# A down projection of a decoder block in Strassen's form, two feature tiles at a time

## The chip, the cores and the metric

The kernel runs on one core of one Trainium2 chip. The time is device microseconds of one launch; three runs of the kernel before give a median of 775.1 us (775.02 to 776.29). The profile is one more execution, which took 774.55 us.

## The reference, cut to what matters

One decoder block on 512 tokens of width 1024, all in float32: norm, two attention mixers side by side, gates, an output projection, then the dense feed-forward part, and a last norm. The change lies in the last product of the feed-forward part, `@ w_down`.

```python
h = rmsnorm(x, norm_ffn[layer])
x = x + (jax.nn.silu(h @ w_gate[layer]) * (h @ w_up[layer])) @ w_down[layer]
return rmsnorm(x, norm_final)
```

`h` is 512 x 1024, `w_gate` and `w_up` are 1024 x 2816, and `w_down` is 2816 x 1024. So the last product has 512 rows (tokens), 1024 columns and a sum over 2816 features.

## The kernel before, in words

**Three matmuls for a float32 product.** TensorE is fed the type fp32r. A float32 operand m is split in two: hi is a copy of m by ScalarE in that type, and lo = m - hi is a subtraction. A product is then hi·hi + lo·hi + hi·lo, three matmuls into one PSUM bank (`mm3`, L200 to L203; L201, L202 and L203 are the three).

**How weights come in.** A `Chunk` (L132 to L178) takes a weight tile of 128x512 float32 (256 KB) by a DMA on SyncE's queue into one of RAW=5 buffers (L153); ScalarE writes `whi` (L172), and VectorE and GpSimd take turns at `wlo` (L164, `PLO` at L108). There are WB=8 buffers each of whi and wlo, so that no split is made until TensorE has read the tile that lay in its buffer.

**Stages.** Up to about 405 us the projections, the two attentions and the output projection; from there the gate and up products (L1007 to L1034, to 645 us); the down projection (L1038 to L1055, 645 to 765 us); and the end of the last norm. The span is 772.8 us.

**Gate and up.** The loop takes feature tiles of 128 features in pairs. For each pair and each of the two weights, TensorE does 2 x 8 `mm3`; the result is features x tokens, a tile of 128x512. VectorE scales g and u (L1016, L1025), ScalarE applies Silu (L1017), VectorE multiplies u by g (L1026), and the result is split in ah (ScalarE, L1032) and al (VectorE, L1033). These 22 pairs of tiles stay in SBUF as the stationary operands of what follows.

**Down.** Eight PSUM banks, `po[b, h]`, hold the output: four blocks b of 128 tokens, two halves h of 512 columns. For each of the first 18 features f, two weight tiles come (h = 0, 1), and TensorE does `mm3` for all b and h, 24 matmuls; the last `LAST = 4` features are done block by block, so that the norm of a block can begin while the next is computed. Then `x1[b][h]`, the residual, is added (L1057), squared and summed (ScalarE, L1060), scaled, and stored.

Engines run their own instructions in the order in which the scheduler of the framework has put them, and wait for one another through semaphores. That order is fixed when the kernel is built; it follows the order of the code and a priority of each instruction, and what the framework's own estimates hold to be ready. Buffers come from pools: `kp` has K2=39 slots of 128x512 under the tag `k2`, in which the operands h2 of gate and up (16 slots), the residual x1 (8) and some of the ah and al lie.

Of the kernel before, what the change touches and what calls it, by code (L numbers as in the profile page):

```python
# [38 lines left out]
def hybrid_block(ctx: ExitStack, tc: tile.TileContext, x, norm_mix, w_in, w_up_a, w_up_b, w_out,  # L39
# [968 lines left out]
    for f in range(0, NF, 2):
        G = []
        W = chunk(wg, [(f * P, 256)])  # L1010
        for j in range(2):
# [7 lines left out]
        W = chunk(wu, [(f * P, 256)])  # L1019
        for j in range(2):  # L1020
# [6 lines left out]
            if f < NFP:  # L1027
                hi, lo = fp.tile([P, 512], F32R, name=f"ah{f + j}"), fp.tile([P, 512], F32R, name=f"al{f + j}")
            else:
                tag = "y" if f + j >= NF - 2 else "rp" if f + j == NF - 3 else "k2"  # L1030
                hi, lo = [kp.tile([P, 512], F32R, tag=tag, bufs={"y": YB, "rp": 2, "k2": K2}[tag], name=f"a{n}{f + j}") for n in "hl"]
            nc.scalar.activation(hi, u, AF.Copy)  # L1032
            nc.vector.tensor_tensor(lo, u, hi.bitcast(F32), op=ALU.subtract)  # L1033
            actT.append((hi, lo))  # L1034
# [5 lines left out]
    LAST = 4  # L1040
    W = {}
    for f in range(NF):
        for h in range(2):
            W[f, h] = chunk(wd[f * P:(f + 1) * P], [(512 * h, 512)], kts=1, per=1)[0]
        if f < NF - LAST:
            for b in range(NB):
                for h in range(2):
                    mm3(po[b, h], (actT[f][0][:, b * P:(b + 1) * P], actT[f][1][:, b * P:(b + 1) * P]), W[f, h], f == 0, False)
    for i in range(2):
        nc.gpsimd.tensor_scalar(gF[:, i * 512:(i + 1) * 512], gF[:, i * 512:(i + 1) * 512], 0.0625, 1.0, op0=ALU.mult, op1=ALU.mult)  # L1050
    for b in range(NB):
        v = None
        for h in range(2):
            for f in range(NF - LAST, NF):
                mm3(po[b, h], (actT[f][0][:, b * P:(b + 1) * P], actT[f][1][:, b * P:(b + 1) * P]), W[f, h], False, f == NF - 1)  # L1055
# [3 lines left out]
            jk = fp.tile([P, 512], F32, tag="g", bufs=3, name="jk")  # L1059
# [50 lines left out]
```

## Time and profile before

| | before |
|---|---|
| median of 3 runs | 775.1 us (775.02 to 776.29) |
| profiled execution | 774.55 us |
| its span (first to last instruction) | 772.8 us |
| mean granted TensorE clock | 0.993 of full speed |
| TensorE busy | 744.1 us, 96% |
| VectorE / ScalarE / GpSimd busy | 435.6 / 352.6 / 281.4 us |
| HBM read / written | 68.46 MB / 2.10 MB |

Busy time of TensorE is the time in which at least one matmul is between its start and its modelled end; matmuls overlap, so that one lasts 0.39 us while the next starts after 0.227. Where the table of stretches has a granted clock of 1.00, TensorE ran at its upper level (2.4 GHz); 0.50 is the lower level (1.2 GHz).

### The profile page before, as it was taken

The page shows a single profiled execution, that of the slowest core. Times are in us where ns is not written, and L with a number is a line of the kernel's source. Part 1 is how long each engine was busy: PE and PEld are TensorE (multiplying, and loading weights), DVE is VectorE, ACT ScalarE, POOL GpSimd, SP SyncE. Part 2 cuts the span into 40 slices and gives each one's busy share as a digit, 9 for nine tenths or more (in the row PEclk, how much of TensorE's full clock was granted, in tenths as well). Part 3 has the DMA queues.
Part 4 walks back from the last instruction along what each step waited for, and adds up shares of the span by engine and source line. Part 5 has one row for each costly group of instructions (what it writes and reads, how often), then busy time and mean ns, then how long its engine had stood idle before and what let it go on. Part 6 is the DMA issues. An engine that isn't in the chain of part 4 may idle for free.

```text
span 772.8 us, 10634 instructions
## 1 busy us (share of the span) xinstructions
PE 744.1 (96%) x3621; PEld 625.2 (81%) x3621; DVE 435.6 (56%) x910; ACT 352.6 (46%) x722; POOL 281.4 (36%) x263
## 2 busy tenths in 40 slices
PE   8988998988999999999999999999999999999995
PEld 7977887886888888888887888888888888888884
DVE  5789989997766557765334344344433343222235
ACT  7366566655666667533425333333333333121233
POOL 2653656645545455422121222222222222222223
PEclk9999999999999999999999999999999999999999
DMA  8352433322432221533232332233223333323202
GB/s 278 80 137 54 102 91 88 89 76 69 117 88 70 73 66 55 176 112 107 82 106 59 109 103 88 83 109 109 84 85 105 109 101 90 105 86 109 83 14 109
DMA packets 68502, 74.53 MB, mean 96 GB/s; under 512 B 5392, under 2 KB 55584, under 8 KB 68448
## 3 DMA queue, kind: packets, MB, share of 16 engines
q1 hardware_dynamic: 68448, 73.86, 32.7%
q8 instruction: 28, 0.46, 0.2%
q14 instruction: 26, 0.21, 0.1%
HBM read 68.46 MB, written 2.10 MB: 91 GB/s over the span
## 4 chain that ended last, share of the span: by engine, by line
PE 82%; DVE 10%; ACT 3%; issue 2%; DMA 1%; SPq 0%; POOL 0%; ACTq 0%; DVEq 0%; POOLq 0%
PE o L202 5%; PE u L203 5%; PE o L203 5%; PE u L202 5%; PE u L201 5%; PE o L201 5%; PE g L203 5%; PE g L202 5%; PE g L201 5%; PE gate L201 3%; PE gate L202 3%; PE gate L203 3%; PE x L203 2%; PE x L201 2%; PE x L202 2%
## 5 line engine op out<-in xcount | busy, mean ns | idle before, releaser
L164 POOL TENSOR_TENSOR wlo<-raw,whi 128x512 fp32r<-128x512 f32 (+1 forms) x156 | 206.1, 1331 | 386.6 <-ACT whi L172 376.4
L172 ACT ACTIVATE whi<-raw 128x512 fp32r<-128x512 f32 (+1 forms) x242 | 149.6, 625 | 240.1 <-PE u L203 70.9
L164 DVE TENSOR_TENSOR wlo<-raw,whi 128x512 fp32r<-128x512 f32 x86 | 71.9, 836 | 128.3 <-ACT whi L172 127.8
L201 PE MATMUL g<-h2h,whi 128*128 128x512 f32 x176 | 68.7, 390 | 0.0
L203 PE MATMUL g<-h2l,whi 128*128 128x512 f32 x176 | 68.7, 390 | 0.0
L202 PE MATMUL g<-h2h,wlo 128*128 128x512 f32 x176 | 68.6, 390 | 0.0
L201 PE MATMUL u<-h2h,whi 128*128 128x512 f32 x176 | 68.5, 389 | 0.0
L202 PE MATMUL u<-h2h,wlo 128*128 128x512 f32 x176 | 68.5, 389 | 0.0
L203 PE MATMUL u<-h2l,whi 128*128 128x512 f32 x176 | 68.5, 389 | 0.0
L201 PE MATMUL o<-whi,ah 128*128 128x512 f32 x176 | 68.5, 389 | 0.0
L202 PE MATMUL o<-whi,al 128*128 128x512 f32 x176 | 68.5, 389 | 0.0
L203 PE MATMUL o<-wlo,ah 128*128 128x512 f32 x176 | 68.5, 389 | 0.0
L684 POOL TENSOR_SCALAR sm<-sm,st 128x256 f32<-128x256 f32 (+3 forms) x64 | 40.0, 632 | 62.4 <-DVE st L683 52.1
L201 PE MATMUL gate<-hTh,whi 128*128 128x512 f32 x128 | 51.6, 403 | 0.0
L203 PE MATMUL gate<-hTl,whi 128*128 128x512 f32 x128 | 50.2, 392 | 0.0
L202 PE MATMUL gate<-hTh,wlo 128*128 128x512 f32 x128 | 50.1, 391 | 0.0
L679 ACT ACTIVATE sm<-sm,st 128x256 f32<-128x256 f32 (+3 forms) x64 | 35.6, 557 | 23.3 <-DVE st L678 23.1
L1025 DVE TENSOR_TENSOR u<-u,rb 128x512 f32<-128x512 f32 x22 | 15.2, 692 | 52.4 <-PE u L203 52.4
L201 PE MATMUL slot<-hTh,whi 128*128 128x512 f32 x104 | 41.7, 401 | 1.8 <-DVE va L563 1.1
L201 PE MATMUL proj<-whi,hTh 128*128 128x256 f32 (+1 forms) x128 | 38.4, 301 | 2.8 <-DVE va L563 1.2
L202 PE MATMUL slot<-hTh,wlo 128*128 128x512 f32 x104 | 40.8, 392 | 0.0
L203 PE MATMUL slot<-hTl,whi 128*128 128x512 f32 x104 | 40.7, 391 | 0.0
(268 smaller groups left out, 1627.0 us busy)
## 6 DMA issues: line engine op xcount, KB each, us to landing
raw<-in_w_in SPq DMA_DIRECT2D x54, 256.0 KB, 3.0
raw<-in_w_gate SPq DMA_DIRECT2D x44, 256.0 KB, 2.9
raw<-in_w_up SPq DMA_DIRECT2D x44, 256.0 KB, 2.9
raw<-in_w_down SPq DMA_DIRECT2D x44, 256.0 KB, 2.8
x<-in_x SPq DMA_DIRECT2D x16, 256.0 KB, 4.0
raw<-in_w_in SPq DMA_DIRECT2D x32, 128.0 KB, 2.5
raw<-in_w_out SPq DMA_DIRECT2D x16, 256.0 KB, 2.6
sw<-raw SPq DMA_DIRECT2D x50, 64.0 KB, 2.0
```

What stands on the lines that cost most here:

```text
L164: eng.tensor_tensor(lo, raw, hi.bitcast(F32), op=ALU.subtract)
L172: nc.scalar.activation(hi, raw, AF.Copy)
L201: nc.tensor.matmul(o, l[0], r[0], start=start, stop=False)
L202: nc.tensor.matmul(o, l[1], r[0], start=False, stop=False)
L203: nc.tensor.matmul(o, l[0], r[1], start=False, stop=stop)
L679: nc.scalar.activation(sm, sm, AF.Exp, bias=st[:, 0:1], scale=-1.0, accum_out=st[:, 1:2])
L684: nc.gpsimd.tensor_scalar(sm, sm, st[:, 2:3], 1.0, op0=ALU.mult, op1=ALU.mult)
L1025: nc.vector.tensor_tensor(u, p_, rb2, op=ALU.mult)
```

## The change

Nine of the eleven pairs of feature tiles of the down projection (the first 18 features) are computed in Strassen's form (Winograd's variant). For a pair, the activations are seen as a 2x2 matrix of blocks: two halves of the tokens (256 each) by two feature tiles; the weights as a 2x2 matrix: two feature tiles by two column halves. Seven block products take the place of eight; each block product is two token blocks of `mm3`, six matmuls.

What stands for the operands:

- In the gate and up loop, the products u·g of a pair go to one tile `ops` of eight parts of 256 tokens (L1042 in the changed file), and four VectorE subtractions or additions of 128x256 make S1, S2, S3 and S5. (A11, A22) and (S1, S2) are split in hi and lo and stay in SBUF, as before (three pairs in the pool `k2`, the others in `fp`); A12, S3 and S5 (128x768 float32, 384 KB) are written to DRAM, unsplit. The tag `g` has 2 buffers in place of 3.
- **Phase 1** does four of the seven products of all nine pairs, into eight banks. Its weights are r11 and three sums, each made by one VectorE addition from the one before (L1101, L1103, L1105), and split.
- **Between the phases** four banks are copied to SBUF (c1, c5) and two more are added to (V), and the four copied are started anew.
- **Phase 2** does the other three products. For each pair it reads `ra` (128x512) and `rb` (128x256) back from DRAM, splits them, takes three weight tiles from DRAM once more and makes one sum.
- Then the parts are added to the residual `x1`, and the last four features are done as before.

The lines of the diff that matter here:

```diff
-            nc.vector.tensor_tensor(u, u, G[j], op=ALU.mult)
+            if ops is not None:
+                to = ops[:, 0:5:4, :] if j else ops[:, 3:8:4, :]
+                nc.vector.tensor_tensor(to, halves(u), halves(G[j]), op=ALU.mult)
+                continue
...
+        A12, S3, S5, A11, A22, S1, S2, A21 = [ops[:, i] for i in range(8)]
+        nc.vector.tensor_tensor(S1, A21, A22, op=ALU.subtract)
+        nc.vector.tensor_tensor(S2, S1, A11, op=ALU.subtract)
+        nc.vector.tensor_tensor(S3, A11, A21, op=ALU.subtract)
+        nc.vector.tensor_tensor(S5, A12, S2, op=ALU.add)
+        spill = dram.tile([P, 768], F32, name=f"spill{pair}")
+        nc.sync.dma_start(spill, ops[:, 0:3].rearrange("p i c -> p (i c)"))
...
+    def wd_split(raw):
+        hi = wp.tile([P, WMAX], F32R, tag="whi", bufs=WB, name="whi")
+        lo = wp.tile([P, WMAX], F32R, tag="wlo", bufs=WB, name="wlo")
+        nc.scalar.activation(hi, raw, AF.Copy)
+        nc.vector.tensor_tensor(lo, raw, hi.bitcast(F32), op=ALU.subtract)
+        return hi, lo
+    def product(b0, h, a, o, w, start, stop):
+        for i in range(2):
+            c = slice(o + i * P, o + (i + 1) * P)
+            mm3(po[b0 + i, h], (a[0][:, c], a[1][:, c]), w, start, stop)
+    for pair in range(NS):
+        fl = (pair == 0, pair == NS - 1)
+        r11, r12, r22, r21 = wd_blocks(pair, ((0, 0), (0, 1), (1, 1), (1, 0)), pair == 0)
+        w11 = wd_split(r11)
+        nc.vector.tensor_tensor(r12, r11, r12, op=ALU.add)
+        u1 = wd_split(r12)
+        nc.vector.tensor_tensor(r22, r12, r22, op=ALU.add)
+        u2 = wd_split(r22)
+        nc.vector.tensor_tensor(r21, r22, r21, op=ALU.add)
+        u4 = wd_split(r21)
+        straight, sums = opA[pair]
+        product(0, 0, straight, 0, w11, *fl)
+        product(0, 1, sums, 0, u1, *fl)
+        product(2, 0, sums, 256, u2, *fl)
+        product(2, 1, straight, 256, u4, *fl)
+    c1, c5, V = [[k2(name=f"{n}_{i}") for i in range(2)] for n in ("c1", "c5", "V")]
+    for i in range(2):
+        nc.scalar.activation(c1[i], po[i, 0], AF.Copy)
...
+        nc.vector.tensor_tensor(V[i], po[2 + i, 0], c1[i], op=ALU.add)
+    for pair in range(NS):
+        ra, rb = k2(name="ra"), k2(name="rb")[:, :256]
+        nc.sync.dma_start(ra, opB[pair][:, 0:512])
+        nc.sync.dma_start(rb, opB[pair][:, 512:768])
+        a = store_pair(ra, "a", lambda n: k2(F32R, n))
+        s5 = store_pair(rb, "s5", lambda n: k2(F32R, n)[:, :256])
+        r21, r22, r12 = wd_blocks(pair, ((1, 0), (1, 1), (0, 1)), False)
+        w21 = wd_split(r21)
+        w22 = wd_split(r22)
+        nc.vector.tensor_tensor(r12, r12, r22, op=ALU.add)
+        u3 = wd_split(r12)
+        product(0, 0, a, 0, w21, pair == 0, False)
+        product(0, 1, s5, 0, w22, pair == 0, False)
+        product(2, 0, a, 256, u3, pair == 0, pair == NS - 1)
...
+    for i in range(2):
+        for o, y in ((x1[i][0], c1[i]), (x1[i][1], c5[i])):
+            if y is c5[i]:
+                nc.vector.tensor_tensor(y, y, V[i], op=ALU.subtract)
+            nc.vector.tensor_tensor(o, o, y, op=ALU.add)
...
-    for f in range(NF):
+    for f in range(NF - LAST, NF):
```

TensorE, the first rows of the down projection. Before, the tiles o_6468, o_6469, o_6470 and so on are the banks `po[0,0]`, `po[0,1]`, `po[1,0]` ..., and the stationary operands are ah and al of feature 0:

```order
L203 MATMUL u<-h2l_4583,whi 128x512
L201 MATMUL o_6468<-whi,ah_4751 128x512
L202 MATMUL o_6468<-whi,al_4752 128x512
L203 MATMUL o_6468<-wlo,ah_4751 128x512
L201 MATMUL o_6469<-whi,ah_4751 128x512
L202 MATMUL o_6469<-whi,al_4752 128x512
```

After, at the same place, o_6533 and o_6535 are `po[0,0]` and `po[1,0]`, o_6534 and o_6536 are `po[0,1]` and `po[1,1]`; a_3h, a_3l are hi and lo of (A11, A22), and a_5h, a_5l those of (S1, S2):

```order
L203 MATMUL u<-h2l_4583,whi 128x512
L201 MATMUL o_6533<-whi,a_3h 128x512
L202 MATMUL o_6533<-whi,a_3l 128x512
L203 MATMUL o_6533<-wlo,a_3h 128x512
L201 MATMUL o_6535<-whi,a_3h 128x512
L202 MATMUL o_6535<-whi,a_3l 128x512
L203 MATMUL o_6535<-wlo,a_3h 128x512
L201 MATMUL o_6534<-whi,a_5h 128x512
```

All rows of TensorE ahead of these are the same in both; a weight tile is now used by two banks in succession, where it was used by four. In the whole program TensorE has 54 rows fewer (3459 and 3405).

TensorE, from phase 1 to phase 2 (only in the changed kernel). o_6537 to o_6540 are the banks `po[2,0]`, `po[2,1]`, `po[3,0]`, `po[3,1]`; ah, al belong to `ra`, s5h, s5l to `rb`:

```order
L203 MATMUL o_6539<-wlo,a_5h 128x512
L201 MATMUL o_6538<-whi,a_3h 128x512
L202 MATMUL o_6538<-whi,a_3l 128x512
L203 MATMUL o_6538<-wlo,a_3h 128x512
L201 MATMUL o_6540<-whi,a_3h 128x512
L202 MATMUL o_6540<-whi,a_3l 128x512
L203 MATMUL o_6540<-wlo,a_3h 128x512
L201 MATMUL o_6533<-whi,ah 128x512
L202 MATMUL o_6533<-whi,al 128x512
L203 MATMUL o_6533<-wlo,ah 128x512
```

Between the last matmul of phase 1 and the first three of phase 2 stands nothing; the second reads al and the third reads wlo.

VectorE, in the down projection before: its subtractions for wlo (those that GpSimd does not do) stand alone until the first block of tokens is done.

```order
L1026 TENSOR_TENSOR u<-u,g 128x512
L1033 TENSOR_TENSOR al_6464<-u,ah_6463 128x512
L164 TENSOR_TENSOR wlo<-raw,whi 128x512 x18
L1057 TENSOR_TENSOR x_0_3977<-o_6468,x_0_3977 128x512
```

VectorE after, from the end of phase 1 on. c_0_7000 and c_1_7001 are c1, c_0_7002 and c_1_7003 are c5, the tiles x_ are parts of the residual:

```order
L1088 TENSOR_TENSOR wlo<-wraw,whi 128x512 x10
L1143 TENSOR_TENSOR x_0_3977<-x_0_3977,c_0_7000 128x512
L1143 TENSOR_TENSOR x_0_3981<-x_0_3981,c_1_7001 128x512
L1119 TENSOR_TENSOR V_7004<-o_6537,c_0_7000 128x512
L1119 TENSOR_TENSOR V_7005<-o_6539,c_1_7001 128x512
L1142 TENSOR_TENSOR c_0_7002<-c_0_7002,V_7004 128x512
L1142 TENSOR_TENSOR c_1_7003<-c_1_7003,V_7005 128x512
L1143 TENSOR_TENSOR x_1_3979<-x_1_3979,c_0_7002 128x512
L1143 TENSOR_TENSOR x_1_3983<-x_1_3983,c_1_7003 128x512
L1025 TENSOR_TENSOR al<-ra,ah 128x512
L1025 TENSOR_TENSOR s5l<-rb,s5h 128x256
L1088 TENSOR_TENSOR wlo<-wraw,whi 128x512 x2
```

Two V and six additions to c5 and x1 stand ahead of the first al and the first wlo of phase 2. GpSimd has no subtraction in either phase until the weights of the last four features.

## Rows read from the trace of the kernel before

**Rows 1.** From the page: busy time of each engine with its share of the span, and the chain of work that ended last, by engine.

```profile
PE 744.1 (96%) x3621; PEld 625.2 (81%) x3621; DVE 435.6 (56%) x910; ACT 352.6 (46%) x722; POOL 281.4 (36%) x263
...
PE 82%; DVE 10%; ACT 3%; issue 2%; DMA 1%; SPq 0%; POOL 0%; ACTq 0%; DVEq 0%; POOLq 0%
```

**Rows 2.** Busy time by stretch: gate and up, down projection, end. After the stretch and its length: busy us (and instructions) of PE, PEld, DVE, ACT, POOL, then the granted clock, the DMA share and GB/s.

```profile
416.20:645.00 228.80, 228.80 (x1011) 189.47 (x1010) 92.74 (x126) 80.09 (x128) 54.76 (x43) 1.00 0.33 96
645.00:765.00 120.00, 119.91 (x530) 98.95 (x528) 36.78 (x55) 32.82 (x59) 32.61 (x26) 1.00 0.26 85
765.00:772.80 7.80, 0.00 (x0) 0.00 (x0) 2.68 (x8) 1.65 (x4) 2.08 (x2) 0.77 0.33 122
```

**Rows 3.** The tile o (the eight banks of the down projection): its matmuls by line, with their count, duration in ns, and first and last start.

```profile
L201 PE MATMUL o<-whi,ah x176: 389/389/389, 645.1 to 764.1; 128*128 128x512 f32 x176
...
L202 PE MATMUL o<-whi,al x176: 389/389/389, 645.3 to 764.3; 128*128 128x512 f32 x176
...
L203 PE MATMUL o<-wlo,ah x176: 388/389/389, 645.5 to 764.5; 128*128 128x512 f32 x176
```

**Rows 4.** Timeline of TensorE as the down projection begins (start, duration).

```profile
644.62 0.39 PE L202 MATMUL u<-h2h,wlo 128*128 128x512 f32 x1
644.85 0.39 PE L203 MATMUL u<-h2l,whi 128*128 128x512 f32 x1
645.07 0.39 PE L201 MATMUL o<-whi,ah 128*128 128x512 f32 x1
645.30 0.39 PE L202 MATMUL o<-whi,al 128*128 128x512 f32 x1
```

**Rows 5.** The waits of the down projection: who waited for whom, us in total, times, longest.

```profile
DVE wlo L164 <- ACT whi L172: 73.6, 18, 4.3
ACT whi L172 <- PE o L202: 64.4, 16, 4.2
```

**Rows 6.** Groups by line and form: VectorE's subtraction of the weights in gate and up (first row), in the down projection (second) and in the whole kernel (third), busy us and mean ns of one; its smaller form of 256 columns elsewhere (fourth); ScalarE's split of weights from 412 us on (fifth); GpSimd's subtraction from 412 us on (sixth).

```profile
L164 DVE TENSOR_TENSOR wlo<-raw,whi 128x512 fp32r<-128x512 f32 x43 | 29.6, 689 | 29.6 <-ACT whi L172 29.1
...
L164 DVE TENSOR_TENSOR wlo<-raw,whi 128x512 fp32r<-128x512 f32 x19 | 23.3, 1228 | 73.6 <-ACT whi L172 73.6
...
L164 DVE TENSOR_TENSOR wlo<-raw,whi 128x512 fp32r<-128x512 f32 x86 | 71.9, 836 | 128.3 <-ACT whi L172 127.8
...
L698 DVE TENSOR_TENSOR ptl<-pT,pth 128x256 fp32r<-128x256 f32 x16 | 6.7, 418 | 2.6 <-ACT pth L697 2.4
...
L172 ACT ACTIVATE whi<-raw 128x512 fp32r<-128x512 f32 x123 | 77.7, 632 | 176.1 <-PE u L203 70.9 <-PE o L202 64.4 <-PE g L203 24.8
...
L164 POOL TENSOR_TENSOR wlo<-raw,whi 128x512 fp32r<-128x512 f32 x62 | 80.5, 1298 | 262.3 <-ACT whi L172 262.3
```

**Rows 7.** Timeline of VectorE: operations of 128x512 in succession, in gate and up.

```profile
624.23 0.69 DVE L164 TENSOR_TENSOR wlo<-raw,whi 128x512 fp32r<-128x512 f32 x1
624.84 0.68 DVE L1026 TENSOR_TENSOR u<-u,g 128x512 f32<-128x512 f32 x1
...
639.83 0.69 DVE L1025 TENSOR_TENSOR u<-u,rb 128x512 f32<-128x512 f32 x1 [4.03 <-PE u L203]
640.56 0.69 DVE L1026 TENSOR_TENSOR u<-u,g 128x512 f32<-128x512 f32 x1
```

**Rows 8.** One subtraction on GpSimd (first row) and one on VectorE (second) that overlap, in the down projection.

```profile
650.56 1.30 POOL L164 TENSOR_TENSOR wlo<-raw,whi 128x512 fp32r<-128x512 f32 x1 [4.59 <-ACT whi L172]
...
651.20 1.21 DVE L164 TENSOR_TENSOR wlo<-raw,whi 128x512 fp32r<-128x512 f32 x1 [2.53 <-ACT whi L172]
```

**Rows 9.** The last matmul of the down projection and the VectorE operation that reads its bank.

```profile
764.52 0.39 PE L203 MATMUL o<-wlo,ah 128*128 128x512 f32 x1
...
764.95 0.69 DVE L1057 TENSOR_TENSOR x<-o,x 128x512 f32<-128x512 f32 x1 [0.29 <-PE o L203]
```

**Rows 10.** The DMA engines as the kernel begins, in two stretches (the columns are those of rows 2), and the issues of the weights of the down projection: KB each and median us to landing.

```profile
0.00:20.00 20.00, 16.60 (x119) 15.30 (x120) 12.24 (x34) 14.70 (x41) 4.67 (x12) 1.00 0.79 272
8.00:16.00 8.00, 7.64 (x63) 7.23 (x63) 7.26 (x22) 7.00 (x23) 0.32 (x1) 1.00 1.01 378
...
raw<-in_w_down SPq DMA_DIRECT2D x44, 256.0 KB, 2.8
```

**Rows 11.** Timeline of TensorE at two places where it waits twice within a few us (in brackets the wait and what ended it), and after each of them the stretch that follows, in the columns of rows 2.

```profile
60.69 0.45 PE L613 MATMUL dots<-idx0h,idx 128*128 128x384 f32 x1 [1.81 <-ACT relu L861]
62.83 0.69 PE L613 MATMUL dots<-idx0h,idx 128*128 128x384 f32 x1 [1.17 <-ACT relu L861]
...
62.90:66.00 3.10, 3.10 (x13) 3.10 (x14) 3.07 (x5) 1.76 (x4) 2.01 (x2) 0.50 0.31 68
...
186.34 0.44 PE L613 MATMUL sc<-qk1A21h,qk0A 128*128 128x384 f32 x1 [1.40 <-DVE st L678]
188.22 0.50 PE L708 MATMUL y<-pth,va 128*128 128x512 f32 x1 [1.15 <-DVE st L683]
...
189.00:192.20 3.20, 3.20 (x15) 3.01 (x13) 1.54 (x7) 3.07 (x9) 2.94 (x3) 0.50 0.29 65
```

More of the change, by code (lines that the diff above doesn't have):

```diff
@@ L1004, in hybrid_block, with halves, store_pair @@
     gF = fp.tile([P, D], F32, name="gF")
-    actT = []
+    LAST = 4
+    NS = (NF - LAST) // 2
+    dram = ctx.enter_context(tc.tile_pool(name="dram", bufs=1, space=bass.MemoryType.DRAM))
+    opA, opB, act = [], [], {}
+    def halves(t):
+        return t.rearrange("p (i c) -> p i c", i=2)
+    def store_pair(m, name, alloc):
+        hi, lo = alloc(name + "h"), alloc(name + "l")
+        nc.scalar.activation(hi, m, AF.Copy)
+        nc.vector.tensor_tensor(lo, m, hi.bitcast(F32), op=ALU.subtract)
+        return hi, lo
     for f in range(0, NF, 2):
         G = []
+        pair = f // 2
         W = chunk(wg, [(f * P, 256)])
@@ L1019, in hybrid_block @@
         W = chunk(wu, [(f * P, 256)])
+        ops = fp.tile([P, 8, 256], F32, tag="ops", bufs=1, name="ops") if pair < NS else None
         for j in range(2):
@@ L1025, in hybrid_block @@
             nc.vector.tensor_tensor(u, p_, rb2, op=ALU.mult)
+            if ops is not None:
+                to = ops[:, 0:5:4, :] if j else ops[:, 3:8:4, :]
+                nc.vector.tensor_tensor(to, halves(u), halves(G[j]), op=ALU.mult)
+                continue
             nc.vector.tensor_tensor(u, u, G[j], op=ALU.mult)
[L1027 to L1034, printed above, removed]
+            i = f + j - (NF - LAST)
+            tag, bufs = (("y", YB) if i >= 2 else ("rp", 2) if i == 1 else ("k2", K2))
+            act[f + j] = store_pair(u, f"a{f + j}", lambda n: kp.tile([P, 512], F32R, tag=tag, bufs=bufs, name=n))
+        if ops is None:
+            continue
+        A12, S3, S5, A11, A22, S1, S2, A21 = [ops[:, i] for i in range(8)]
[5 more added lines that the diff above has]
+        nc.sync.dma_start(spill, ops[:, 0:3].rearrange("p i c -> p (i c)"))
+        opB.append(spill)
+        alloc = (lambda n: k2(F32R, n)) if pair < NSK else (lambda n: fp.tile([P, 512], F32R, name=n))
+        opA.append([store_pair(ops[:, i:i + 2].rearrange("p i c -> p (i c)"), f"a{pair}_{i}", alloc) for i in (3, 5)])
     nc.sync.dma_start(gF, bass.AP(tensor=norm_final.tensor, offset=norm_final.offset, ap=[[0, P], [1, D]]))
@@ L1039, in hybrid_block, with wd_blocks @@
     po = {(b, h): banks[2 * b + h](f"o{b}{h}") for b in range(NB) for h in range(2)}
-    LAST = 4
+    def wd_blocks(pair, which, from_wp):
+        res = []
+        for r, c in which:
+            t = wp.tile([P, WMAX], F32, tag="raw", bufs=RAW, name="raw") if from_wp else k2(name="wraw")
+            nc.sync.dma_start(t, wd[(2 * pair + r) * P:(2 * pair + r + 1) * P, 512 * c:512 * (c + 1)])
+            res.append(t)
+        return res
+    def wd_split(raw):
[3 more added lines that the diff above has]
+        nc.vector.tensor_tensor(lo, raw, hi.bitcast(F32), op=ALU.subtract)
+        return hi, lo
@@ new lines, in hybrid_block @@
+    c1, c5, V = [[k2(name=f"{n}_{i}") for i in range(2)] for n in ("c1", "c5", "V")]
+    for i in range(2):
+        nc.scalar.activation(c1[i], po[i, 0], AF.Copy)
+    for i in range(2):
+        nc.scalar.activation(c5[i], po[i, 1], AF.Copy)
+    for i in range(2):
+        nc.vector.tensor_tensor(V[i], po[2 + i, 0], c1[i], op=ALU.add)
[13 more added lines that the diff above has]
+        product(2, 0, a, 256, u3, pair == 0, pair == NS - 1)
@@ new lines, in hybrid_block @@
+    for i in range(2):
+        o = x1[2 + i][1]
+        nc.vector.tensor_tensor(o, o, po[2 + i, 0], op=ALU.subtract)
+        o = x1[2 + i][0]
+        nc.vector.tensor_tensor(o, po[2 + i, 0], o, op=ALU.add)
+    for i in range(2):
+        for o, y in ((x1[i][0], c1[i]), (x1[i][1], c5[i])):
+            if y is c5[i]:
+                nc.vector.tensor_tensor(y, y, V[i], op=ALU.subtract)
+            nc.vector.tensor_tensor(o, o, y, op=ALU.add)
+    for i in range(2):
+        o = x1[2 + i][0]
+        nc.vector.tensor_tensor(o, po[2 + i, 1], o, op=ALU.add)
+        nc.vector.tensor_tensor(o, o, V[i], op=ALU.add)
+        o = x1[2 + i][1]
+        nc.vector.tensor_tensor(o, o, c5[i], op=ALU.add)
@@ L1058, in hybrid_block @@
             ss = small.tile([P, 1], F32, name="ss3")
[L1059 removed]
+            jk = fp.tile([P, 512], F32, tag="g", bufs=2, name="jk")
             nc.scalar.activation(jk, o, AF.Square, accum_out=ss)
```

11 lines of the change are left out of this document (4 added, 7 removed).

## The prediction

> **What bounds the kernel now.** I read the page first: TensorE is busy 96% of the span, and 82% of the chain that ended last is TensorE [rows 1]. Then the table of stretches: in the down projection TensorE is busy 119.91 of 120 us at a granted clock of 1.00, VectorE and ScalarE about 37 and 33 us, and the DMA engines a quarter of the time [rows 2]. Then the tile o: 3 x 176 = 528 matmuls, the first starting at 645.1 and the last at 764.5 [rows 3]; so one starts each (764.52 - 645.07) / 527 = 0.2267 us [rows 4, 9]. There is no gap where gate and up pass into down [rows 4]. The waits say it from the other side: the split of the weights waits 64.4 us for TensorE to free a buffer [rows 5]. Work taken from VectorE, ScalarE or DMA would give nothing here; each matmul taken from TensorE gives 0.2267 us, as long as the others keep up.
>
> **What goes.** Seven block products of 6 matmuls replace eight for each of nine pairs: 9 x 6 = 54 matmuls fewer, 54 x 0.2267 = 12.24 us, all on the path.
>
> **Gate and up.** Four VectorE operations of 128x256 are added for each pair, at 0.418 us [rows 6]: 9 x 4 x 0.418 = 15.0 us more beside 92.74 busy us in 228.8 [rows 2]. They stand behind the last product of a pair and nothing on TensorE reads them before 645 us. The tile `ops` is written anew only after the 48 matmuls of the next gate and 24 of the next up, 72 x 0.2267 = 16.3 us later, and its store to DRAM (384 KB) is one transfer where 256 KB land in 2.8 us [rows 10]. I take 0. What hides this is VectorE's idle time; without it the cost is at most the 15.0 us.
>
> **Phase 1, a pair.** TensorE: 24 x 0.2267 = 5.44 us. VectorE: three sums and four subtractions of 128x512. One lasts 0.69 us, but starts follow each other at 0.61 where the second needs nothing from the first, and at 0.73 where it does [rows 7]; 7 operations take 4.3 to 5.1 us. ScalarE: 4 x 0.63 = 2.5 us [rows 6]. DMA: four tiles, 1.05 MB in 5.44 us, 193 GB/s, where 378 were moved in a full stretch [rows 10]. TensorE stays the bound; I take 0.
>
> **Phase 2, a pair.** TensorE: 18 x 0.2267 = 4.08 us. VectorE: five operations of 512 and one of 256 columns, 5 x 0.61 + 0.42 = 3.5, and at 0.69 and a little for the sum that ScalarE must split before VectorE can go on, 3.9 us. ScalarE: 4 x 0.63 + about 0.4 = 2.9 us. DMA: 128x512, 128x256 and three weight tiles are 1.18 MB in 4.08 us, 289 GB/s. All below TensorE, though VectorE by only 0.2 to 0.6 us. I take 0.
>
> **The switch between the phases.** Here a wait is added. Let T be the time at which phase 2's first matmul could start. V[1] reads the bank po[3,0], whose last matmul stands seven before T, at T - 1.59; a reader starts 0.43 us after the start of the last matmul (764.52 and 764.95) [rows 9], so V[1] starts at T - 1.16. Behind it on VectorE stand two c5, two x1, and then al: five starts later at 0.61, T + 1.9, and done 0.69 us after, T + 2.6. The second matmul needs al and was due at T + 0.23: it waits 2.4 us. Then come s5l (0.42) and the first wlo, done at about T + 3.5; the third matmul, due at T + 2.8, waits 0.7 more. TensorE's third product needs u3. Its sum, ScalarE's split of it and the subtraction (0.6 each and a hand-over) still come after the second weight's wlo, so that u3's lo is there at about T + 6.2; the matmul that reads it and the three after it end the pair at T + 7.2 in place of T + 4.08. So the switch costs 3.1 us. From both sides: 2.4, if only al is late and the rest is caught up; 4.0, if the starts follow at 0.73. I take 3.1, the value at the spacing of operations that need nothing from the one before, since the eight in this row alternate between i = 0 and i = 1. After it VectorE gains 0.2 to 0.6 us on TensorE in each pair, and no further wait is expected. Nothing else waits for the queue behind al: ScalarE's splits are bounded by VectorE's own buffers.
>
> **The clock after it.** In two places of the trace TensorE waits twice in a row: 1.81 and 1.17 us, and 1.40 and 1.15 us; after each the granted clock stands at 0.50 (1.2 GHz) for 3.1 to 3.2 us [rows 11]. The switch has waits of 2.4 and 0.7 us and another shorter one. I expect the same fall: some 3.1 us at half speed, 1.5 us lost. From both sides: 0 (no fall) and 3.2 (twice as long).
>
> **The end.** Ten VectorE additions follow phase 2, about 6.1 us at 0.61, ahead of three subtractions for the last four features; the first matmuls of these features use tiles split before, 36 of them or 8.2 us, so the wait is 0. The last norm after 765 us is as before [rows 2].
>
> **Sum.** 774.55 - 12.24 + 3.1 + 1.5 = 766.9 us for the profiled execution, which lay 0.55 us under the median of the runs, 775.1. So 767.4 us as a median.
>
> **A page against the change.** In the first stretch, loads of mostly 256 KB moved 378 GB/s at a DMA share of 1.01 [rows 10]. The Trainium skill, page "SBUF — State Buffer", section "The DMA setup-cost knee", gives 224 GB/s for transfers of 256 KiB, against 341 for 1 MiB. By that figure, as an estimate, a pair of phase 2 would take 1.18 MB / 224 = 5.27 us, 1.19 over TensorE, and nine of them 10.7 us, so that the kernel would take about 778. The row speaks against it as long as several transfers are under way at once.
>
> **Rivals.**
>
> *The clock does not fall.* For it: during the switch matmuls run between the waits. Against it: they did in both places of rows 11 too. 767.4 - 1.5 = 765.9 us.
>
> *DMA is late in phase 2.* It needs 289 GB/s; 272 was the mean of the first 20 us at a share of 0.79, and 378 the most [rows 10]. At 272 a pair takes 4.34 us, 0.26 more, with eight pairs behind the first: +2.1, 769.5 us. Other small waits of this size (a buffer of k2 freed late, DRAM read back late) come to about 772 at most. Much worse is a stream with only two transfers under way: 2 x 262 KB / 2.8 us = 187 GB/s, 6.3 us a pair, +2.2 x 9 = 20, about 787 us. Against that: phase 2 has 39 slots of k2 less 8 for x1, 2 for a18 and 6 for c1, c5, V, so 23, and a pair takes 9, so loads run two pairs ahead, ten transfers.
>
> *VectorE becomes the bound (slower than before).* All subtractions are now on VectorE, and its operations last longer than 0.69 us where GpSimd reads SBUF beside it: 1.21 us beside a GpSimd operation of 1.30 [rows 8], 1.228 on the mean in the down projection, 0.836 over the kernel [rows 6]. At a spacing of 0.836 a pair of phase 1 takes 5.85 us (+0.41), one of phase 2 5 x 0.836 + 0.51 = 4.69 (+0.61), over eight pairs each 8.2 us; the switch grows by seven operations x 0.226 = 1.6. 767.4 + 9.8 = 777.2 us. It is slower than before from a spacing of 0.82 on. Against it: the order has no GpSimd operation in the two phases, and in gate and up the mean was 0.689 with GpSimd at work for a quarter of the time [rows 2, 6].
>
> The Trainium skill, "SBUF — State Buffer", section "Who interferes with whom", says that a VectorE instruction with two SBUF inputs contends with a GpSimd instruction that reads SBUF; by it, too, phases without GpSimd work stay at 0.69.
>
> That the matmuls do not become fewer is no rival: TensorE's rows fell by exactly 54.
>
> **How the numbers follow.** Forecast 0.55 (767.4). No fall of the clock 0.13 (765.9). DMA or other waits of a few us 0.17 (769.5 to 772). VectorE as the bound 0.10 (777, with a fifth of it ending below 774). DMA far behind 0.05 (778 to 787). The range goes from 764.5 (no fall and a switch of 2.4, less 0.7 of scatter) to 773, which leaves some 0.05 below and 0.13 above. 0.2% of 775.1 is 1.55 us, about what a measurement can tell from no change: faster below 773.55, slower above 776.65. Faster 0.55 + 0.13 + 0.17 + 0.02 = 0.87; same 0.04; slower 0.09.
>
> **What the changed profile would show.** TensorE: 474 matmuls of the tile o, at 0.2267 us in both phases, with no wait in phase 1. One group of waits at the switch, about 71 us before the end of the span (nine pairs at 4.08, 3.1 and 1.5 lost, 96 matmuls of the last features, 7.9), "al" and then "wlo" as releasers, 3.1 us in sum; the granted clock near 0.5 for 3 us behind it. VectorE's operations at 0.69 us in both phases; GpSimd without work. DMA at 290 GB/s in phase 2 with weights landing ahead of their splits. Gate and up still ending at 645 us. I am wrong if TensorE waits in every pair of a phase, if VectorE's mean there is over 0.75 us, if gate and up grow, or if the end behind the last matmul is longer than 7.9 us.

## The result and the profile after

The changed kernel takes 769.27 us (median of four runs, 769.24 to 769.57), the kernel before 775.06 us in the same series (774.69 to 776.29): a ratio of 0.9923, with a 95% interval of 0.9906 to 0.9941. The forecast was 767.4 us in a range of 764.5 to 773. The profiled execution of the changed kernel took 769.30 us, with a span of 767.2.

Executions of one kernel differ by 0.3 to 4 us (the four runs of a2 below went from 765.99 to 769.98); those that stand apart by more than 1.5 us have the highest or the lowest mean granted clock of their kernel. Part of the difference lies ahead of the down projection, where TensorE's rows are the same in all kernels: it began between 643.8 and 647.0 us in the profiles below. So every term is read here from stretches of one profile, and the totals only confirm it.

First the tile o in the changed kernel, the waits of TensorE from 645 us on, and the table of stretches (columns as in [rows 2]): phase 1, the first pair of phase 2, the rest of phase 2, the last four features, the end, and the stretch behind the first wait. A row with x2 is two operations in succession.

```profile
L201 PE MATMUL o<-whi,a_3h x36: 389/389/389, 645.1 to 693.3; 128*128 128x512 f32 x36
...
L203 PE MATMUL o<-wlo,ah x36: 389/389/797, 697.6 to 735.3; 128*128 128x512 f32 x36
```

```profile
PE o L202 <- DVE al L1025: 2.2, 1, 2.2
PE o L203 <- DVE wlo L1088: 0.4, 1, 0.4
```

```profile
645.00:694.00 49.00, 49.00 (x217) 40.57 (x217) 37.38 (x61) 23.12 (x40) 0.00 (x0) 1.00 0.59 204
694.00:702.90 8.90, 6.26 (x19) 4.49 (x18) 8.74 (x16) 3.56 (x8) 0.00 (x0) 0.81 0.39 134
702.90:735.50 32.60, 32.60 (x145) 27.00 (x144) 26.09 (x43) 21.84 (x42) 4.25 (x3) 1.00 0.71 228
735.50:759.00 23.50, 21.98 (x97) 17.85 (x96) 19.42 (x44) 8.99 (x22) 8.99 (x7) 1.00 0.13 48
759.00:767.20 8.20, 0.00 (x0) 0.00 (x0) 2.80 (x9) 2.04 (x6) 2.53 (x2) 0.71 0.34 128
...
697.50:701.10 3.60, 3.54 (x9) 2.84 (x10) 3.44 (x7) 2.30 (x5) 0.00 (x0) 0.53 0.74 255
```

Where [rows 3] had matmuls of 389 ns from 645.1 to 764.5, phase 1 and almost all of phase 2 look the same, and only the longest reach 797 ns: they lie at the lower clock behind the switch (0.53). In the whole stage TensorE waits in one place. VectorE had 36.78 busy us in 120 before [rows 2]; now it has 26.09 in 32.6, and GpSimd has none in phase 1.

TensorE at the switch, with the wait in brackets:

```profile
693.80 0.39 PE L203 MATMUL o<-wlo,a_3h 128*128 128x512 f32 x1
694.02 0.39 PE L201 MATMUL o<-whi,ah 128*128 128x512 f32 x1
696.62 0.50 PE L202 MATMUL o<-whi,al 128*128 128x512 f32 x1 [2.21 <-DVE al L1025]
697.55 0.80 PE L203 MATMUL o<-wlo,ah 128*128 128x512 f32 x1 [0.43 <-DVE wlo L1088]
698.15 0.63 PE L201 MATMUL o<-whi,ah 128*128 128x512 f32 x1
```

The second matmul starts 2.60 after the first and the third 0.93 after the second, in place of 0.227: 2.37 + 0.70 = 3.07 us of waits. From the third on the starts are 0.36 to 0.60 apart; the old spacing is back at 701.07. The first matmul of the last four features starts at 735.56, so phase 2 took 41.54 us, where 162 matmuls at 0.2267 take 36.73. The 4.81 us over that are the 3.07 of waits and 1.74 of clock. VectorE there:

```profile
690.09 1.37 DVE L1143 TENSOR_TENSOR x<-x,c 128x512 f32<-128x512 f32 x2 [5.62 <-ACT c L1115]
692.18 1.37 DVE L1119 TENSOR_TENSOR V<-o,c 128x512 f32<-128x512 f32 x2 [0.72 <-PE o L203]
693.47 1.28 DVE L1142 TENSOR_TENSOR c<-c,V 128x512 f32<-128x512 f32 x2
694.67 1.29 DVE L1143 TENSOR_TENSOR x<-x,c 128x512 f32<-128x512 f32 x2
695.88 0.69 DVE L1025 TENSOR_TENSOR al<-ra,ah 128x512 fp32r<-128x512 f32 x1
```

al starts 1.86 us after T = 694.02 (the forecast had 1.9). It is made of ra and ah, and ScalarE wrote ah here:

```profile
692.00 0.62 ACT L1024 ACTIVATE ah<-ra 128x512 fp32r<-128x512 f32 x1
```

So from 692.62 on, for 3.26 us, al waited only for its place on VectorE, behind the additions. But VectorE had also been idle for 5.62 us right ahead of this row of operations, and ScalarE for 5.71 us ahead of its copies of the banks (from 689.46), behind which it wrote ah, while ra lay in SBUF long before (its load was issued at 661.8 us, and none of these loads took over 5.3 us).

The end: the last matmul starts at 757.09, so 10.1 us are left to the end of the span, where 8.3 were before (764.52 to 772.8). VectorE, GpSimd and VectorE again:

```profile
750.21 1.23 DVE L263 SCALAR_TENSOR_TENSOR rs_t<-rs,v 128x1 f32<-128x1 f32 x1
751.47 1.22 DVE L267 SCALAR_TENSOR_TENSOR rs<-rs_t,rs 128x1 f32<-128x1 f32 x1
752.72 0.22 DVE L263 SCALAR_TENSOR_TENSOR rs_t<-rs,v 128x1 f32<-128x1 f32 x1
...
759.50 0.68 DVE L1163 TENSOR_TENSOR x<-o,x 128x512 f32<-128x512 f32 x1
```

```profile
750.13 2.55 POOL L1167 TENSOR_TENSOR x<-x,gF 128x512 f32<-128x512 f32 x2 [0.55 <-ACT jk L1166]
```

The last read of a bank starts 2.41 us after the last matmul, against 0.43 in [rows 9]: VectorE is late, and it is VectorE that TensorE's results now wait for.

### The profile page after: what moved, and what is told of

Read it like the earlier page. It is cut to its first block, busy times and chain, and to the rows that moved or that the text cites. A ratio compares the mean times of both kernels' runs of the same rounds, so it can differ in the third digit from the quotient of the medians.

```text
span 767.2 us, 10936 instructions
## 1 busy us (share of the span) xinstructions
PE 734.3 (96%) x3567; PEld 616.1 (80%) x3567; DVE 502.4 (65%) x1063; ACT 378.3 (49%) x771; POOL 258.2 (34%) x245
## 4 chain that ended last, share of the span: by engine, by line
PE 71%; DVE 9%; ACT 3%; issue 2%; ACTq 0%; DVEq 0%
PE u L201 5%; PE u L203 5%; PE u L202 5%; PE g L203 5%; PE g L201 5%; PE g L202 5%; PE o L203 4%; PE o L201 4%; PE o L202 4%; PE gate L202 3%; PE gate L201 3%; PE gate L203 3%; PE x L203 2%; PE x L201 2%; PE x L202 2%; PE up L201 2%
## 5 line engine op out<-in xcount | busy, mean ns | idle before, releaser
L164 POOL TENSOR_TENSOR wlo<-raw,whi 128x512 fp32r<-128x512 f32 (+1 forms) x138 | 183.0, 1337 | 402.5 <-ACT whi L172 392.3
L172 ACT ACTIVATE whi<-raw 128x512 fp32r<-128x512 f32 (+1 forms) x206 | 126.5, 624 | 164.4 <-PE u L203 70.0
L164 DVE TENSOR_TENSOR wlo<-raw,whi 128x512 fp32r<-128x512 f32 x68 | 49.9, 736 | 66.2 <-ACT whi L172 65.8
L1087 ACT ACTIVATE whi<-wraw 128x512 fp32r<-128x512 f32 x59 | 36.2, 628 | 36.8 <-PE o L202 9.6
L1088 DVE TENSOR_TENSOR wlo<-wraw,whi 128x512 fp32r<-128x512 f32 x59 | 39.6, 687 | 6.7 <-ACT whi L1087 6.3
L203 PEld LDWEIGHTS u<-h2l,whi 128*128 128x128 f32 x176 | 33.0, 188 | 6.9
```

What stands on the lines that cost most here:

```text
L164: eng.tensor_tensor(lo, raw, hi.bitcast(F32), op=ALU.subtract)
L172: nc.scalar.activation(hi, raw, AF.Copy)
L203: nc.tensor.matmul(o, l[0], r[1], start=False, stop=stop)
L1087: nc.scalar.activation(hi, raw, AF.Copy)
L1088: nc.vector.tensor_tensor(lo, raw, hi.bitcast(F32), op=ALU.subtract)
```

## The experiments

Lengths in us, from TensorE's timeline: phase 1 and phase 2 from their first matmul to the first of what follows (48.97 and 36.73 at 0.2267 a matmul), the last four features from their first start to their last (21.54), the end from there to the end of the span.

| kernel | phase 1 | phase 2 | last four | end | median us |
|---|---|---|---|---|---|
| changed kernel | 48.95 | 41.54 | 21.53 | 10.11 | 769.27 |
| a1 prep first | 48.96 | 36.72 | 21.54 | 10.09 | 764.91 |
| a2 weights first | 48.96 | 42.63 | 21.54 | 9.56 | 769.77 |
| a3 both | 48.96 | 36.72 | 21.72 | 10.11 | 765.33 |
| a4 no gain | 48.96 | 39.93 | 21.54 | 7.49 | 763.82 |
| a5 early adds | 48.96 | 36.72 | 21.54 | 8.59 | 763.59 |
| a6 gain split | 48.96 | 36.72 | 21.53 | 8.28 | 763.41 |
| a7 VectorE margin | 48.97 | 40.77 | 22.26 | 8.40 | 768.23 (one) |
| a8 more DMA | 48.96 | 37.46 | 24.23 | 8.68 | 765.16 (one) |
| a9, a10 again | 48.96 | 41.49, 41.42 | 21.53 | 10.08, 10.11 | 769.01, 769.38 (one each) |

### a1: phase 2's first operands ahead of the switch

```diff
+    def prep(pair):
+        ra, rb = k2(name="ra"), k2(name="rb")[:, :256]
...
+        return a, s5, w21, w22, u3
+    ready = {pair: prep(pair) for pair in range(1)}
     c1, c5, V = [[k2(name=f"{n}_{i}") for i in range(2)] for n in ("c1", "c5", "V")]
...
     for pair in range(NS):
-        ra, rb = k2(name="ra"), k2(name="rb")[:, :256]
...
+        a, s5, w21, w22, u3 = ready[pair] if pair in ready else prep(pair)
```

> The changed kernel with the loads and splits of phase 2's first pair written ahead of the copies of the banks c1 and c5, so that VectorE does its al, s5l and three wlo in its idle 5.6 us before them. My theory (the wait at the switch is the place of al and wlo in VectorE's queue, 3.07 us, and the clock falls because of it, 1.71 us): both go, 769.3 - 4.8 = 764.5 us, no TensorE wait over 0.3 us at the switch, granted clock 1.00. Rival 1 (the switch is bound by the sum of VectorE's work, which is not less): the wait moves to the third or a later product, at least 767. Rival 2 (the clock falls at a change of phase whatever the wait): 766.2, with a stretch of granted clock 0.5 to 0.6 still there.

Measured: 764.91 us, ratio 0.9865 (0.9841 to 0.9889). Phase 2 takes 36.72 us. TensorE and then VectorE at the switch, where T is now 695.45:

```profile
695.23 0.39 PE L203 MATMUL o<-wlo,a_3h 128*128 128x512 f32 x1
695.45 0.39 PE L201 MATMUL o<-whi,ah 128*128 128x512 f32 x1
695.68 0.39 PE L202 MATMUL o<-whi,al 128*128 128x512 f32 x1
695.90 0.39 PE L203 MATMUL o<-wlo,ah 128*128 128x512 f32 x1
```

```profile
691.52 1.37 DVE L1149 TENSOR_TENSOR x<-x,c 128x512 f32<-128x512 f32 x2 [1.49 <-ACT c L1130]
693.61 1.37 DVE L1134 TENSOR_TENSOR V<-o,c 128x512 f32<-128x512 f32 x2 [0.72 <-PE o L203]
694.90 1.29 DVE L1148 TENSOR_TENSOR c<-c,V 128x512 f32<-128x512 f32 x2
```

The same additions run at the same place against T. The edit moves ScalarE's splits too: ah is now written at 668.81, and al, s5l and the sum follow on VectorE at 672.45, 676.06 and 679.07, among the operations of phase 1; only the three wlo went into the idle time before the additions, of which 1.49 us are left (the expectation had al and s5l in it as well). Waits and lower clock are both gone, 4.82 us. Rival 1 (the sum of the work bounds the switch) and rival 2 (the clock falls at a change of phase) both fall.

### a2 and a3: the last weights ahead of the ten additions

```diff
+    W = {}
+    for f in range(NF - LAST, NF):
+        for h in range(2):
+            W[f, h] = chunk(wd[f * P:(f + 1) * P], [(512 * h, 512)], kts=1, per=1)[0]
     for i in range(2):
         o = x1[2 + i][1]
         nc.vector.tensor_tensor(o, o, po[2 + i, 0], op=ALU.subtract)
...
-    W = {}
...
```

> The changed kernel with the splits of the weights of the last four features written ahead of the ten additions that follow phase 2. TensorE then takes the last four features bank by bank again. My theory (the end grew by 1.84 us because the first banks end late and close together, so that VectorE lags behind): the end after the last matmul's start goes from 10.1 to 8.3 us, total 767.4. Rival 1 (the ten additions delay the norm whatever their order): the end stays at 10.1, 769.3. Rival 2 (TensorE now waits for the additions or for wlo): the end is 8.3 but TensorE waits 1 us or more in the last four features, 768.4 or more.

> Both edits of the two kernels before. If the two terms are independent, as I hold: 769.3 - 4.8 - 1.8 = 762.7 us. If the end's lag comes from what VectorE did earlier in phase 2 (it has caught up by other means): 764.5, as with the first edit alone.

Measured: a2 769.77 us (0.9917, 0.9887 to 0.9948), a3 765.33 us (0.9869, 0.9846 to 0.9892); the end is 9.56 and 10.11 us. TensorE went almost bank by bank, as it did before the change, and lost at most 0.2 us (a3); my theory of the end, as put for a2, fell, and rival 1 (the additions delay the norm whatever their order) held, with a2's end 0.5 us under the 10.1 that it gave. VectorE and then GpSimd in a3:

```profile
739.86 0.68 DVE L1157 TENSOR_TENSOR x<-x,V 128x512 f32<-128x512 f32 x1
740.46 1.88 DVE L1169 TENSOR_TENSOR x<-o,x 128x512 f32<-128x512 f32 x3
...
744.90 0.90 DVE L263 SCALAR_TENSOR_TENSOR rs_t<-rs,v 128x1 f32<-128x1 f32 x1
745.83 1.21 DVE L267 SCALAR_TENSOR_TENSOR rs<-rs_t,rs 128x1 f32<-128x1 f32 x1
```

```profile
741.98 5.04 POOL L1173 TENSOR_TENSOR x<-x,gF 128x512 f32<-128x512 f32 x4 [6.79 <-ACT jk L1172]
```

Three banks are read in one go once the additions are over; their squares follow at once, and GpSimd then has four multiplications back to back. Beside them two operations on 128x1 take 0.90 and 1.21 us.

That the order on TensorE is not what delays the end shows from the other side too. In the changed kernel the last four features are not done as before: TensorE mixes the matmuls of the first five banks, and their reads start at 743.92, 745.50, 746.41, 748.02 and 749.36, where before the first three were 2.72 us apart (745.91, 748.63, 751.35). The next kernel, a4, has the mixed order as well, and a short end.

### a4: without the multiplication on GpSimd

```diff
-            nc.gpsimd.tensor_tensor(o, o, gF[:, h * 512:(h + 1) * 512], op=ALU.mult)
```

> The changed kernel without GpSimd's multiplication of the result by the gain of the last norm (eight operations of 128x512; the output lacks that factor). Small VectorE operations of 128x1 took 1.23 us in place of 0.2 while such a multiplication ran, two of them, 2.0 us. If these are what VectorE lags by at the end: the last read of a bank starts 0.45 us after its last matmul, end 8.3, total 767.4. If VectorE lags because of its own operations and ScalarE's: the end stays within 0.4 us of 10.1, total 769 or so.

Measured: the end is 7.49 us, 2.62 less than in the changed kernel, with the ten additions where they were; total 763.82 us (0.9852, 0.9820 to 0.9883). The total fell by 5.45 us in all; besides the end, the clock did not fall behind the switch in this execution (1.61 us of phase 2), and the stage began 1.19 us earlier. VectorE:

```profile
747.43 0.21 DVE L263 SCALAR_TENSOR_TENSOR rs_t<-rs,v 128x1 f32<-128x1 f32 x1
747.67 0.16 DVE L267 SCALAR_TENSOR_TENSOR rs<-rs_t,rs 128x1 f32<-128x1 f32 x1
...
754.73 0.69 DVE L1163 TENSOR_TENSOR x<-o,x 128x512 f32<-128x512 f32 x1 [0.53 <-PE o L203]
```

The output of a4 lacks the gain. The two operations take 0.37 us in place of 2.45, and the last read of a bank waits for TensorE again, 0.42 us after the last matmul (754.31). So the 1.83 us are lost on VectorE beside GpSimd. The end is even under the 8.28 of the kernel before, where one such operation of the last block also took 0.64 us.

### a5 and a6: six additions early, and half the multiplications

```diff
-    ready = {pair: prep(pair) for pair in range(1)}
+    ready = {pair: prep(pair) for pair in range(2)}
...
+        for fn in adds[max(pair - 2, 0) * 1:max(pair - 2 + 1, 0) * 1]:
+            fn()
```

`adds` are the additions of po[2 + i, 1], V and c5 to x1[2 + i], written one behind each pair from the third on; in the profile of a5 the scheduler has them at 697.05 to 701.7 us, early in phase 2. a6 adds to this:

```diff
-            nc.gpsimd.tensor_tensor(o, o, gF[:, h * 512:(h + 1) * 512], op=ALU.mult)
+            if h == 1:
+                nc.gpsimd.tensor_tensor(o, o, gF[:, 512:1024], op=ALU.mult)
...
-        nc.vector.tensor_scalar(x1[b][0], x1[b][0], rs3, None, op0=ALU.mult)
+        nc.vector.scalar_tensor_tensor(x1[b][0], x1[b][0], rs3, gF[:, 0:512], op0=ALU.mult, op1=ALU.mult)
```

> As the kernel with phase 2's preparation first, now for its first two pairs, and six of the ten additions that followed phase 2 (those that need nothing of phase 2) are written ahead of it. If the end grew because these additions hold up VectorE as the last four features begin: four are left (2.4 us in place of 6.0), the end goes from 10.1 to 8.3 to 8.8 us, total 763.3 (764.9 - 1.6). If it is GpSimd's multiplications that lengthen VectorE's small operations, whatever comes before: the end stays at 9.5 to 10.1. A wait in phase 2's first pairs (six additions more in its first 8 us) would show as phase 2 longer than 36.7 us; I expect none.

> As the kernel with the early additions, and the gain of the last norm is multiplied in by VectorE's last operation for the first column half, so that GpSimd has four multiplications in place of eight. If VectorE's small operations of 128x1 beside GpSimd (1.23 in place of 0.2 us) are what the end lost: the end goes to 7.8 to 8.3 us, total 762.6. If not: as the kernel with the early additions alone, or 0.2 us more for the longer last operation.

Measured: a5 763.59 us (0.9836, 0.9806 to 0.9866), end 8.59; a6 763.41 us (0.9834, 0.9807 to 0.9861), end 8.28. Both ends lie where they were expected (a6's total, expected at 762.6, does not); between the two totals no difference can be told. GpSimd in a5, as the last features begin:

```profile
737.73 1.30 POOL L1181 TENSOR_TENSOR x<-x,gF 128x512 f32<-128x512 f32 x1 [4.31 <-ACT jk L1180]
739.32 1.29 POOL L1181 TENSOR_TENSOR x<-x,gF 128x512 f32<-128x512 f32 x1 [0.28 <-ACT jk L1180]
741.45 1.29 POOL L1181 TENSOR_TENSOR x<-x,gF 128x512 f32<-128x512 f32 x1 [0.84 <-ACT jk L1180]
745.39 1.29 POOL L1181 TENSOR_TENSOR x<-x,gF 128x512 f32<-128x512 f32 x1 [2.65 <-ACT jk L1180]
```

The multiplications stand apart again, and fewer of VectorE's small operations fall beside one. With 3.6 us fewer additions in front, four operations of VectorE remain ahead of the wlo. Phase 2 holds the six additions at no cost (36.72). Both kernels are faster than the kernel before and than the changed one: their intervals do not touch the changed kernel's 0.9906 to 0.9941.

### a7 and a8: how near the other bounds are

```diff
+        if pair:
+            for w, r in ((w21, r21), (w22, r22)):
+                nc.vector.tensor_tensor(w[1], r, w[0].bitcast(F32), op=ALU.subtract)
```

```diff
+        for r in range(2 if pair else 0):
+            t = k2(name="extra")
+            nc.sync.dma_start(t, wd[(2 * pair + r) * P:(2 * pair + r + 1) * P, 0:512])
```

> As the kernel with phase 2's preparation first, but the subtraction for the first two weights of a pair of phase 2 is done twice (from the second pair on): two VectorE operations of 128x512 more in a pair. VectorE's pair then takes 5 x 0.61 + 0.42 + 2 x 0.61 = 4.7 us against TensorE's 4.08: if VectorE was 0.6 us under the bound, phase 2 grows by 0.6 x 8 = 5 us less what was prepared ahead, 40 to 42 us in place of 36.7. If it had more room (operations overlap more than I read), under 38. If it had none, 45 or more.

> As the kernel with phase 2's preparation first, with two weight tiles of 256 KB more loaded for each pair of phase 2 from the second on, and not used: 1.70 MB in place of 1.18 for a pair. In phase 2 as it is, the DMA engines were busy 0.71 of the time at 228 GB/s, so 1.0 would be 321 GB/s, and a pair 5.3 us: phase 2 would grow by up to 8 us, less what two pairs' loads ahead give (4 us). At 378 GB/s a pair takes 4.5 us, and the growth is 0 to 3 us. If only the latency of a transfer matters, no growth at all.

Measured: with two VectorE operations more in each of eight pairs, phase 2 takes 40.77 us, within 40 to 42; VectorE is the bound there, busy 34.72 of 35 us, and its al of one pair starts 4.67 us after that of the pair before (700.89, 705.56, 710.24 and on). With two weight tiles more, phase 2 takes 37.46 (0.74 more), and the last four features 24.23 (2.7 more), since their splits come late: TensorE waits 1.2 us for wlo from GpSimd and 0.4 for a whi. Each of the two was run once. The stretch of phase 2 in a7 and then in a8:

```profile
697.00:732.00 35.00, 33.41 (x141) 25.72 (x140) 34.72 (x61) 17.00 (x34) 0.00 (x0) 1.00 0.62 192
```

```profile
697.00:732.00 35.00, 34.52 (x149) 27.05 (x148) 28.44 (x46) 22.10 (x41) 3.02 (x3) 1.00 0.83 288
```

In a8 288 GB/s at a share of 0.83 came through over 35 us, with TensorE waiting little; so the DMA rival had its limit above the 228 GB/s that the changed kernel moved there. Where the limit lies is not settled. Phase 2 itself grew by 0.74 us, within the 0 to 3 of 378 GB/s; with the last features it is 3.4, between that and the 4 that 321 GB/s left (8 less what is loaded ahead). The unused tiles also take two more buffers of `k2` for each pair, and the run does not part that from the rate. The ends of a7 and a8 are 8.40 and 8.68 us without any edit there. That TensorE took longer over the last features (0.7 and 2.7 us), so that VectorE caught up, can't be all of it in a7, where the end is 1.7 us shorter: there no operation of 128x1 took more than 0.84 us. So how many of them meet a GpSimd multiplication also hangs on how the instructions happen to fall.

### a9, a10 and a11: the clock again, and five pairs

a9 and a10 are the changed kernel, unchanged. a11 is a1 with

```diff
-    NS = (NF - LAST) // 2
+    NS = 5
```

and a loop of the kernel before (eight `mm3` a feature) for the features 10 to 17, between phase 2 and the last four.

> The changed kernel once more, for the clock behind the switch. The waits (2.4 and 0.7 us late) should be the same. If they alone decide, phase 2 is 41.5 us again (1.7 us lost at the lower clock). If what the clock does also hangs on something that differs between executions, it can be 39.9 (nothing lost, as in the run without the gain) up to 42.6 (2.8 lost, as in the run with the weights first).

> The same kernel a further time, with the same two readings: 41.5 us again, or another value between 39.9 and 42.6.

> As the kernel with phase 2's preparation first, but five pairs in the form with seven products in place of nine, and the other eight features of these done with eight products between phase 2 and the last four. If the gain is 6 matmuls of 0.2267 us for each pair: 4 x 1.36 = 5.4 us more from the first matmul of the down projection to the last than with nine pairs (phases 36.72 + 48.96 + 21.76 there), so 112.9 us; total about 770.3 less or more 1. If most of the gain came from elsewhere (fewer weight tiles, VectorE in GpSimd's place), 109 or less.

Measured: phase 2 is 41.49 and 41.42 us in a9 and a10, with starts 2.59 and 0.94 apart at the switch in both, so 3.07 us of waits and 1.69 and 1.62 of clock. a2 and a4 had the same two distances, and lost 2.83 and 0.13 us to the clock. a4 and a2 right after the waits:

```profile
695.40:699.00 3.60, 3.13 (x12) 2.36 (x13) 3.44 (x7) 1.39 (x4) 0.00 (x0) 1.00 0.60 212
```

```profile
697.30:703.20 5.90, 5.80 (x14) 4.54 (x15) 5.65 (x11) 3.52 (x8) 0.00 (x0) 0.50 0.45 160
```

So the waits alone do not decide how long the clock stays low. The profiles hold a second case of this, the later place of [rows 11], which runs before anything that was edited. All thirteen profiles have the same two waits there, of 1.38 to 1.41 and of 1.14 or 1.15 us. Behind them the granted clock fell to 0.50 or 0.51 in seven (the kernel before, the changed kernel, a3, a6, a9, a10, a11), and stayed at 1.00 in six (a1, a2, a4, a5, a7, a8). Here is a4, with the stretch that [rows 11] shows at 0.50:

```profile
186.64 0.45 PE L613 MATMUL sc<-qk1A21h,qk0A 128*128 128x384 f32 x1 [1.40 <-DVE st L678]
188.52 0.50 PE L708 MATMUL y<-pth,va 128*128 128x512 f32 x1 [1.14 <-DVE st L683]
...
189.00:192.20 3.20, 3.20 (x22) 2.81 (x21) 1.84 (x7) 3.07 (x9) 2.93 (x3) 1.00 0.21 46
```

It is no state of a whole execution either: a2, which had no fall there, lost the most behind the switch, and a3 and a6, which had one, run at 1.00 where a1's edit took the waits away. What decides is open. At the switch it may go with the kernel: the six runs of the changed kernel, a9 and a10 among them, lie at 769.01 to 769.57, and both of a4 are short (763.62, 764.03).

a11 takes 113.47 us from the first matmul of the stage to the last (expected 112.9). Its 498 matmuls make 497 steps, 112.67 us at 0.2267, and the other 0.8 is lost at one place, where TensorE waits for a wlo: a pair is worth its 6 matmuls and nothing else. The total, 770.37 us (expected 770.3), fits in part by chance, since the end is 2 us shorter than a1's: 8.11 us, though it has the ten additions too: there 192 matmuls lie between them and the last four features.

## Why the prediction was right, and where it was off

| term of the sum | forecast | measured |
|---|---|---|
| 54 matmuls | -12.24 | -12.24 |
| waits at the switch | 3.1 (2.4 to 4.0) | 3.07 |
| the clock after it | 1.5 (0 to 3.2) | 1.74 |
| the end | 0 | 1.83 |
| outside the span | 0 | 0.35 |
| profiled execution | 766.9 | 769.3 |

**The matmuls.** 119.45 us from first to last start before, 48.95 + 41.54 + 21.53 = 112.02 after, of which 4.81 are the switch: 107.21, so 12.24 less. The gain of a pair is confirmed by a11.

**Gate and up, phase 1, phase 2 at cost 0.** Right. From 404 to 646 us TensorE's only wait is the same in both profiles, one of 0.9 us for rs_r, and the stage starts at 645.07 in both; from there on TensorE waits nowhere but at the switch; VectorE's operations took 687 ns on the mean. The margin of VectorE, put at 0.2 to 0.6 us a pair, is shown by a7: a pair with two operations more (1.2 us) takes VectorE 4.67 us, so one without takes about 3.5, and the room was 0.6. Phase 2 grew by only 0.5 us a pair ((40.77 - 36.72) / 8) because the first pairs had been prepared ahead.

**The switch.** Right in its mechanism and its size: the two V begin at 692.18, 1.84 us before T, and al starts six operations later at 695.88, 0.62 us each. What the forecast did not look for is that the wait was not needed: VectorE stood idle 5.6 us ahead of it and ScalarE 5.7, as a1 shows.

**The clock.** It fell as in [rows 11], and a1, without waits, shows no fall. The size, 1.74, 1.69 and 1.62 us in three executions, is near the 1.5; 0.13 and 2.83 in two other kernels with the same waits show that the bounds of 0 and 3.2 were needed, and that a value so near was in part luck. [rows 11] was one execution: behind its later place six of thirteen profiles show no fall, so these rows bore less than the forecast put on them.

**The end: the step that failed.** "The last norm after 765 us is as before" was the mistake. The forecast asked only whether TensorE would wait for the ten additions (it did not), and left out that VectorE itself does the norm of the first blocks in that time. Its own last sign of being wrong came: from the end of the last matmul (757.48) to the end of the span are 9.7 us, not 7.9. The additions put it 6 us behind, the norms of the first blocks come close together, GpSimd's multiplications run back to back, and two of VectorE's operations of 128x1 last 1.23 and 1.22 us in place of 0.22 and 0.16: 2.07 us, of which 1.83 reach the end. a4 takes away GpSimd's part and the lag is gone; a5 takes away six of the additions and 1.5 us of it is gone. The Trainium skill, page "SBUF — State Buffer", section "Who interferes with whom", has the rule: a VectorE instruction with two SBUF inputs contends with a GpSimd instruction that reads SBUF; one with at most one does not, outside the 2-port modes, which tensor_scalar can enter. The trace agrees, as VectorE and GpSimd at the end of a5 show:

```profile
755.94 0.16 DVE L260 RECIPROCAL rs<-rs 128x1 f32<-128x1 f32 x1 [0.27 <-ACT rs L259]
756.14 0.64 DVE L263 SCALAR_TENSOR_TENSOR rs_t<-rs,v 128x1 f32<-128x1 f32 x1
```

```profile
755.50 1.26 POOL L1181 TENSOR_TENSOR x<-x,gF 128x512 f32<-128x512 f32 x1 [0.34 <-ACT jk L1180]
```

The reciprocal, with one input, takes 0.16 us inside the multiplication; the operation with two inputs ends at 756.78, when the multiplication does (756.76). So do the two of the changed kernel: they end at 751.44 and 752.69, the row of two multiplications at 752.68. But not every operation with one tensor input is spared. In the kernel before, one of 128x512 that also reads a scalar took 1.34 us beside a multiplication, where it takes 0.47 to 0.49 elsewhere in that norm; that fits the exception, though no view names the mode (VectorE, then GpSimd):

```profile
753.12 1.34 DVE L1066 TENSOR_SCALAR x<-x,rs 128x512 f32<-128x512 f32 x1
...
752.88 1.30 POOL L1061 TENSOR_TENSOR x<-x,gF 128x512 f32<-128x512 f32 x1 [1.43 <-ACT jk L1060]
```

The forecast weighed this for phases 1 and 2 and not for the norm.

**Outside the span.** 774.55 - 772.8 = 1.75 us before and 769.3 - 767.2 = 2.1 after. It goes with the end: 1.8 in the five profiles whose end is 8.4 us or shorter (before, a4, a6, a7, a11), 2.1 in the eight others. No view shows what lies there, so the cause stays open.

**The rivals.** VectorE as the bound did not come about: no GpSimd operation ran beside the two phases until 730 us, and the mean stayed at 0.69. DMA moved 228 GB/s over most of phase 2 at a share of 0.71, not the 290 of the forecast (the loads of the first pairs were issued in phase 1, from 661.8 us on), and TensorE did not wait for it. The 224 GB/s for 256 KiB of the Trainium skill (page "SBUF — State Buffer", section "The DMA setup-cost knee"), which spoke against the change, is passed by the 288 of a8; here the measurement decides. With the waits of the switch in place, the clock stayed up in a4 alone of the five profiles.
